# Reading the moving columns of every product as two halves in turn

## The chip, the cores and the metric

The kernel runs on one core of one Trainium2 chip. The metric is the device time of one execution, in microseconds (us). Engines are named as the profile names them: PE is TensorE (PEld its weight loads), DVE is VectorE, ACT is ScalarE, POOL is GpSimd, SP is SyncE, whose queue issues most DMAs.

## What is computed

One encoder layer on 512 tokens of width 1024, in float32. Two token mixers run side by side on the same input `h`, are merged by sigmoid gates, and a gated feed-forward net follows:

```python
proj = h @ w_in[l]
...
o_a = windowed_gqa_sink(qa, ka, va, a_sink[l]).astype(h.dtype)
o_b = dilated_mixture(qb, kb, vb).astype(h.dtype)
gates = jax.nn.sigmoid(h @ w_gate[l] + b_gate[l])
g_a, g_b = jnp.split(gates, N_BRANCH, axis=-1)
mixed = g_a * (o_a @ w_br_a[l]) + g_b * (o_b @ w_br_b[l])
y = mixed @ w_out[l]
h = layer_norm(DN_ALPHA * h + y, ln1_g[l], ln1_b[l])
f = (jax.nn.silu(h @ w_ff_gate[l]) * (h @ w_ff_up[l])) @ w_ff_down[l]
h = layer_norm(DN_ALPHA * h + f, ln2_g[l], ln2_b[l])
```

Mixer A has 16 query heads over 4 key heads and a window of 128 tokens to both sides. Mixer B has three groups of 4 heads with the window and dilation (128,1), (512,4) and (2048,16). The feed-forward width is 2816.

## The kernel before

**Split products.** Each float32 operand is cut into a high part `h` and a low part `l`, both of type float32r, by a copy (`copy`, L320 to L324, usually on ACT) and a subtraction (L348 and L371 on weights, L427 on `x`, L1213 later, all on DVE). A product is then three matmuls that add up in one PSUM bank: high by high, high by low, low by high. The stationary side has 128 columns (one weight load per matmul), the moving side 512 or 256. The places are these:

- `feat_k` (L442) multiplies weights by the moving tokens for projections, gates and the branch outputs: L452 to L454, 512 columns.
- `token_values` (L655) does it the other way round, tokens stationary and weights moving: L672 to L674.
- `scores` (L594, matmuls L601 and L602) and L828 make attention scores; L767, L768, L895 and L932 multiply probabilities with values.
- `tok_major` (L1098) does the output projection and the end of the down projection: L1110 to L1112.
- `Quad.product` (L1315) does gate and up projection, four 128-row steps at a time with 256 moving columns: L1323 to L1325. A block of 2 by 2 matrices takes seven products there, with sums of operands formed ahead and sums of results behind.
- `Chunk.step` (L1520) does most of the down projection in the same way: L1533 to L1535, 512 columns.

**Readers of PSUM.** `rotate` (L470: L472 and L474) applies the rotary turn; L750, L812, L835 and L838 add masks and take the row minimum; L779, L907 and L938 add two halves of an attention output; the gates are read at L958, the branch outputs at L1065 and L1077, layer norm sums at L1134; the quads copy (L322 on ACT, through `keep`), add (L1213, through `tt` and `plus`) and multiply (L1347, `minus_product`). Transposes on PE (L634, L701, L716, L1180) write banks that others read in plain order.

**Order.** The order on the engines is made when the program is built: `Program.run` (L167) is a list scheduler. Each `op` has a price (`act`, `dve` and `pe`, L268 to L277), a priority and the buffers that it holds; an operation starts on its engine when its inputs are priced as ready and its buffers fit, smallest priority first. Copies may go to ACT or DVE (`cp_alts`). The price of a matmul before is

```python
def pe(n):
    return max(0.109, 0.0133 + n / 2400)
```

in us for n moving columns. These prices decide the order, not the time on the chip. `copy`'s price for PSUM and `dve`'s price for 512 columns (0.60 us) are untouched by the change.

The work runs in this sequence: input, projections and both mixers, with gates in between (to 345 us), branch outputs (to about 400 us), output projection and layer norm (to about 460 us), the feed-forward quads and chunks (to about 745 us), the last of the down projection and the second layer norm.

Of the kernel before, what the change touches and what calls it, by code (L numbers as in the profile page):

```python
# [15 lines left out]
P = 128  # L16
# [259 lines left out]
def pe(n):  # L276
    return max(0.109, 0.0133 + n / 2400)  # L277
# [3 lines left out]
def hybrid_layer(ctx: ExitStack, tc: tile.TileContext, wpack, xT, xtok, sink, bgate,  # L281
# [134 lines left out]
    for j in range(KD):  # L416
        st, ap = slot(F32, "xs"), FIRST["x"][j]

        for c0, c1 in ((0, S // 2), (S // 2, S)) if j == 0 else ((0, S),):
            w, sk = c1 - c0, (st, c0)  # L420
            th, tl = [(b, j, c0) if j == 0 else (b, j) for b in (xh4[j // 4], xl4[j // 4])]
            eng, dma = (ACT, nc.scalar) if j == 0 and c0 == 0 else (SP, nc.sync)
            op([(eng, 0.4 if eng == ACT else 0.73 * w / S)], lambda e, j=j, st=st, dma=dma, c0=c0, c1=c1: dma.dma_start(
                st.t[:, c0:c1], xT[j, :, c0:c1]), writes=[sk], abs_prio=ap, moves=0.73 * w / S if eng == ACT else 0.0)
            op(cp_alts(w), lambda e, j=j, st=st, c0=c0, c1=c1: copy(e, xh[j]()[:, c0:c1], st.t[:, c0:c1]),
               reads=[sk], writes=[th], abs_prio=ap)
            op([(DVE, dve(w))], lambda e, j=j, st=st, c0=c0, c1=c1: nc.vector.tensor_tensor(  # L427
                xl[j]()[:, c0:c1], st.t[:, c0:c1], f32(xh[j]()[:, c0:c1]), op=ALU.subtract), reads=[sk, th],
               writes=[tl], abs_prio=ap)
# [12 lines left out]
    def feat_k(ps, wu, k, mov, toks, nk=KD, col=None, n0=0, n1=S, begins=True, split=False):  # L442
# [27 lines left out]
    def rotate(ps):  # L470
        R, Sh = slot(), slot()
        op([(DVE, dve(S))], lambda e: nc.vector.tensor_tensor(R.t, ps.t, cosT.t, op=ALU.mult),  # L472
           reads=[ps, cosT], writes=[R], prio=EV)
        op([(DVE, dve(S, extra=0.1))], lambda e: nc.vector.stream_shuffle(Sh.t, ps.t, SHUF), reads=[ps], writes=[Sh],  # L474
# [119 lines left out]
    def scores(o_of, q, qc, k, kc, n):  # L594
# [4 lines left out]
        def go():  # L599
            o = o_of()  # L600
            mm(o, qt.t[:, qc:qc + P], kt.t[:, kc:kc + n], start=True, stop=False, skip_group_check=True)  # L601
            mm(o, qt.t[:, qc:qc + P], kl.t[:, kc:kc + n], start=False, stop=True, skip_group_check=True)  # L602
# [4 lines left out]
    def turned_values(u, nt, turn_by=0, done=None):  # L607
# [3 lines left out]
        for i in range(2):  # L611
# [28 lines left out]
    def value_split(pb, c0=0):  # L640
# [3 lines left out]
        s = lambda: pb.t[:, c0:c0 + 256].rearrange("p (h c) -> p h c", h=4)  # L644
# [10 lines left out]
    def token_values(u):  # L655
# [11 lines left out]
        for k in range(KD):  # L667
            wh, wl = k_tile(k)
            for r, ps in enumerate(acc):
                def go(e, ps=ps, k=k, wh=wh, wl=wl, r=r):  # L670
                    a, b = xh[k]()[:, r * P:(r + 1) * P], xl[k]()[:, r * P:(r + 1) * P]
                    mm(ps.t, a, wh.t, start=(k == 0), stop=False)  # L672
                    mm(ps.t, a, wl.t, start=False, stop=False)
                    mm(ps.t, b, wh.t, start=False, stop=(k == KD - 1))  # L674
# [3 lines left out]
        for ps in acc:  # L678
            for g in range(2):
                res[g].append(value_split(ps, 256 * g))  # L680
# [53 lines left out]
    def unit_a(g, b, qs, kk, vs):  # L734
# [6 lines left out]
        for h in range(4):  # L741
# [9 lines left out]
                out=p.t[:, :n], in0=sb.t[:, :n], in1=mA.t[:, m0:m0 + n], scale=-0.125,  # L751
# [10 lines left out]
        for j, kb in enumerate(kbs):  # L762
            hh, ll = turned_probs([lambda h=h, j=j: ps_[h].t[:, j * P:(j + 1) * P] for h in range(4)], ps_)

            def pv(e, j=j, kb=kb, hh=hh, ll=ll):
                v = vs[kb].t.rearrange("p (h c) -> p h c", h=4)[:, g, :]
                mm(o.t, v, hh.t, start=(j == 0), stop=False)  # L767
                mm(o.t, v, ll.t, start=False, stop=(j == len(kbs) - 1))  # L768
# [3 lines left out]
        op(cp_alts(S, True), lambda e: copy(e, t.t[0:64], o.t[64:128]), reads=[o], writes=[t])  # L772

        def add(e):
            for h in range(4):
# [3 lines left out]
                nc.vector.tensor_tensor(dst, o.t[0:64, c].rearrange("p (r i) -> p r i", r=4),  # L779
# [4 lines left out]
    def unit_b(hs, q, k, v0, v1, v2):  # L784
# [12 lines left out]
        for half in range(2):  # L797
# [10 lines left out]
            for b in (2 * half, 2 * half + 1):  # L808
# [4 lines left out]
                       out=pn[half].t[:, c + w0:c + w1], in0=sb.t[:, c + w0:c + w1], in1=mB.t[:, w0:w1],  # L813
# [8 lines left out]
        for half in range(2):  # L822
            for r in (2 * half, 2 * half + 1):
                sb, c = bank("s"), (r % 2) * 256

                def go(e, sb=sb, r=r, c=c):
                    for g in (1, 2):
                        mm(sb.t[:, (g - 1) * 256:g * 256], q[g][0].t[:, r * P:(r + 1) * P],  # L828
                           k[g][r // 2].t[:, c:c + 256], start=True, stop=True, skip_group_check=True)
# [3 lines left out]
                two = lambda sb=sb: sb.t.rearrange("p (g a i) -> p g a i", g=2, a=2)  # L833
# [51 lines left out]
        for half in range(2):  # L885
# [5 lines left out]
            def pv(e, half=half, xs=xs, od=od):  # L891
                for n, x in enumerate(xs):
                    for g, vs in ((1, v1), (2, v2)):
                        v = vs[2 * half + n].t.rearrange("p (h c) -> p h c", h=4)[:, hs, :]
                        mm(od.t[:, n * 256:(n + 1) * 256], v, x.t[:, (g - 1) * 256:g * 256],  # L895
# [6 lines left out]
            part = lambda od=od: od.t.rearrange("p (r a i) -> p r a i", r=2, a=2)  # L902
# [50 lines left out]
    def gate(f, put=False):  # L953
# [4 lines left out]
        op([(ACT, act(S, True, 1))], lambda e: nc.scalar.activation(t.t, ps.t, AF.Identity, bias=bg.t[:, f:f + 1]),  # L958
# [101 lines left out]
    for f in range(8):  # L1060
# [4 lines left out]
        mark = op([(DVE, dve(S))], lambda e, f=f, ps=ps: nc.vector.tensor_tensor(gz[f].t, gz[f].t, ps.t, op=ALU.mult),  # L1065
# [5 lines left out]
    for f in range(8):  # L1071
# [5 lines left out]
        op([(DVE, dve(S))], lambda e, f=f, ps=ps: nc.vector.tensor_tensor(gz[8 + f].t, gz[8 + f].t, ps.t, op=ALU.mult),  # L1077
# [20 lines left out]
    def tok_major(nk, last, us_of, u0, g, b, finish, fine, alpha=ALPHA, between=None):  # L1098
# [4 lines left out]
        def kmm(k, t, j, c0, c1, us, wu):  # L1103
# [3 lines left out]
            def go(e):  # L1107
                a0, a1 = us[0].t[:, t * P:(t + 1) * P], us[1].t[:, t * P:(t + 1) * P]
                o = ps.t[:, c0:c1]
                mm(o, a0, wh.t[:, c0:c1], start=(k == 0), stop=False, skip_group_check=True)  # L1110
                mm(o, a0, wl.t[:, c0:c1], start=False, stop=False, skip_group_check=True)  # L1111
                mm(o, a1, wh.t[:, c0:c1], start=False, stop=(k == nk - 1), skip_group_check=True)  # L1112
# [11 lines left out]
        for t in range(NR):  # L1124
# [3 lines left out]
            for n, (j, c0, c1) in enumerate(pieces):  # L1128
                ps, z = acc[t, j], xt[t, j]
                for k, us, wu in res:  # L1130
# [4 lines left out]
                    z.t[:, c0:c1], z.t[:, c0:c1], alpha, ps.t[:, c0:c1], op0=ALU.mult, op1=ALU.add),  # L1135
# [541 lines left out]
```

## Time and profile before

| | |
|---|---|
| time, median of 3 runs (lowest, highest) | 787.1 us (786.98, 789.37) |
| the profiled execution, first to last instruction | 783.3 us; its time as the runs are timed is not listed apart |
| PE busy, matmul records | 770.7 us (98%), 4477 |
| DVE busy | 669.8 us (86%) |
| ACT busy | 448.8 us (57%) |
| granted clock of TensorE over the span | 0.997 |
| DMA | 124.89 MB, 159 GB/s in the mean |

A matmul's duration in the profile is longer than the distance to the next one, since matmuls are pipelined and their ends are modelled. What a matmul costs in a stream is read from the starts of its neighbours in the timeline. In the chain of waits, which follows the end of the program back to its start, a piece is charged only the time until the next piece begins.

### The profile page before, as it was taken

How to read it: one execution, taken by the hardware profiler on the slowest of the kernel's cores; microseconds unless marked ns; L12 is line 12 of the kernel's file. 1: busy time of each engine (PE TensorE's matmuls, PEld its weight loads, DVE VectorE, ACT ScalarE, POOL GpSimd, SP SyncE). 2: the span in 40 equal slices, each digit the busy share in tenths (PEclk: the TensorE clock that was granted, in tenths of full speed). 3: DMA queues.
4: the chain of work that ended last, by engine and by line, in shares of the span. 5: the costliest groups of instructions: out<-in, count | busy, mean ns of one | idle time of the engine just before them, and what ended most of it. 6: DMA issues, size and time to landing. Idle time of an engine off the chain costs nothing.

```text
span 783.3 us, 13444 instructions
## 1 busy us (share of the span) xinstructions
PE 770.7 (98%) x4477; PEld 677.5 (86%) x4477; DVE 669.8 (86%) x1445; ACT 448.8 (57%) x1009; POOL 103.5 (13%) x272
## 2 busy tenths in 40 slices
PE   9999999999999999999999999999999999999995
PEld 6888888888888888878878899999999999999984
DVE  5888998989697799578698898798998989898977
ACT  5656576765664663569433565656566555565710
POOL 0010000100002500340020011111112201212100
PEclk9999999999999999999999999999999999999998
DMA  8644543425527057649755368665977967967402
GB/s 273 222 124 136 133 123 95 121 87 157 158 64 210 27 137 194 182 162 311 230 116 137 81 212 193 162 162 149 230 226 184 223 160 201 239 168 177 106 28 80
DMA packets 71652, 124.89 MB, mean 159 GB/s; under 512 B 8864, under 2 KB 12832, under 8 KB 71584
## 3 DMA queue, kind: packets, MB, share of 16 engines
q1 hardware_dynamic: 61648, 106.08, 43.4%
q0 software_dynamic: 9792, 17.83, 14.1%
q8 instruction: 35, 0.57, 0.3%
q14 instruction: 33, 0.27, 0.1%
q10 hardware_dynamic: 144, 0.13, 0.0%
HBM read 105.40 MB, written 4.46 MB: 140 GB/s over the span
## 4 chain that ended last, share of the span: by engine, by line
PE 87%; DVE 7%; DMA 3%; ACT 2%; issue 1%; SPq 1%; DVEq 0%; ACTq 0%
PE ps L452 10%; PE ps L453 10%; PE ps L454 10%; PE ps L1323 9%; PE ps L1325 9%; PE ps L1324 9%; PE ps L1534 4%; PE ps L1533 4%; PE ps L1535 4%; PE ps L701 3%; PE ps L1110 2%; PE ps L1112 2%; PE ps L1111 2%; PE ps L602 1%; PE ps L601 1%
## 5 line engine op out<-in xcount | busy, mean ns | idle before, releaser
L322 ACT ACTIVATE sl<-sl 128x512 fp32r<-128x512 f32 (+3 forms) x397 | 218.5, 585 | 87.8 <-DVE sl L478 32.8
L1213 DVE TENSOR_TENSOR sl<-sl,sl 128x512 fp32r<-128x512 f32 (+3 forms) x294 | 166.4, 608 | 7.2 <-ACT sl L322 6.3
L322 ACT ACTIVATE sl<-ps 128x256 f32<-128x256 f32 (+4 forms) x195 | 83.9, 444 | 115.1 <-PE ps L1325 71.9
L452 PE MATMUL ps<-x,sl 128*128 128x512 f32 (+1 forms) x337 | 134.7, 400 | 0.0
L453 PE MATMUL ps<-x,sl 128*128 128x512 f32 (+1 forms) x337 | 132.2, 392 | 0.2 <-DVE x L427 0.2
L454 PE MATMUL ps<-x,sl 128*128 128x512 f32 (+1 forms) x337 | 131.6, 391 | 0.0
L1323 PE MATMUL ps<-sl,sl 128*128 128x256 f32 x352 | 99.8, 283 | 0.2 <-ACT sl L322 0.2
L348 DVE TENSOR_TENSOR sl<-sl,sl 128x512 fp32r<-128x512 f32 x130 | 87.3, 684 | 14.8 <-ACT sl L322 10.0
L1325 PE MATMUL ps<-sl,sl 128*128 128x256 f32 x352 | 99.6, 283 | 0.0
L1324 PE MATMUL ps<-sl,sl 128*128 128x256 f32 x352 | 99.6, 283 | 0.0
L454 PEld LDWEIGHTS ps<-x,sl 128*128 128x128 f32 x337 | 63.7, 189 | 13.7
L1323 PE MATMUL ps<-x,sl 128*128 128x256 f32 x264 | 74.7, 283 | 0.0
L1325 PE MATMUL ps<-x,sl 128*128 128x256 f32 x264 | 74.7, 283 | 0.0
L1324 PE MATMUL ps<-x,sl 128*128 128x256 f32 x264 | 74.7, 283 | 0.0
L453 PEld LDWEIGHTS ps<-x,sl 128*128 128x128 f32 x337 | 63.8, 189 | 11.1 <-DVE x L427 0.9
L452 PEld LDWEIGHTS ps<-x,sl 128*128 128x128 f32 x337 | 63.8, 189 | 10.8 <-ACT x L322 0.5
L336 POOL DMA_DIRECT2D sl<-wpack x44 | 39.3, 904 | 248.5 <-DMA sl<-wpack 107.7
L1323 PEld LDWEIGHTS ps<-sl,sl 128*128 128x128 f32 x352 | 67.5, 192 | 1.1 <-ACT sl L322 0.6
L1324 PEld LDWEIGHTS ps<-sl,sl 128*128 128x128 f32 x352 | 67.5, 192 | 0.4
L1325 PEld LDWEIGHTS ps<-sl,sl 128*128 128x128 f32 x352 | 67.5, 192 | 0.0
L1324 PEld LDWEIGHTS ps<-x,sl 128*128 128x128 f32 x264 | 50.6, 192 | 0.6
L1323 PEld LDWEIGHTS ps<-x,sl 128*128 128x128 f32 x264 | 50.6, 192 | 0.6
(143 smaller groups left out, 1598.3 us busy)
## 6 DMA issues: line engine op xcount, KB each, us to landing
sl<-wpack SPq DMA_DIRECT2D x243, 256.0 KB, 3.8
sl<-sl SPq DMA_DIRECT2D x108, 128.0 KB, 2.3
wf<-wpack SPq DMA_DIRECT2D x51, 256.0 KB, 4.8
sl<-wpack POOLq DMA_DIRECT2D x44, 256.0 KB, 5.6
wf<-wpack POOLq DMA_DIRECT2D x24, 256.0 KB, 5.2
gz<-sl SPq DMA_DIRECT2D x9, 256.0 KB, 2.2
sl<-gz SPq DMA_DIRECT2D x9, 256.0 KB, 5.1
sl<-xtok SPq DMA_DIRECT2D x8, 256.0 KB, 5.6
```

The lines of the kernel that those rows point to most:

```text
L322: nc.scalar.activation(dst, src, AF.Copy)
L336: op([(POOL, 1.0)], lambda e: nc.gpsimd.dma_start(b.t, src2, accum_op=ALU.add), reads=[b], writes=[b], prio=prio, moves=1.65)
L348: op([(DVE, dve(S))], lambda e: nc.vector.tensor_tensor(l.t, src.t, f32(h.t), op=ALU.subtract), reads=[src, h], writes=[l], prio=prio, abs ...
L452: mm(o, a, x0, start=(k == 0 and begins), stop=False, skip_group_check=split)
L453: mm(o, a, x1, start=False, stop=False, skip_group_check=split)
L454: mm(o, b, x0, start=False, stop=(k == nk - 1), skip_group_check=split)
L1213: op([(DVE, dve(w))], lambda e: nc.vector.tensor_tensor(dst(), x(), y(), op=o), reads=reads, writes=writes, prio=prio)
L1323: mm(o, wh, bh[k](), start=(first and k == 0), stop=False, skip_group_check=True)
L1324: mm(o, wh, bl[k](), start=False, stop=False, skip_group_check=True)
L1325: mm(o, wl, bh[k](), start=False, stop=(k == 3), skip_group_check=True)
L1533: mm(ps.t, x0, w[0].t, start=(first and m == 0), stop=False, skip_group_check=True)
L1534: mm(ps.t, x0, w[1].t, start=False, stop=False, skip_group_check=True)
```

## The change

Every matmul of a product, except the windowed value product L932, reads its moving columns in another order: instead of columns 0, 1, 2, ... it reads column 0, column n/2, column 1, column n/2 + 1, and so on. Three helpers make the access patterns: `pairs` for the matmul's moving operand, `back` for a PSUM result (its columns now stand with a step of two), `halves` for a tile in SBUF that is read or written along with such a result as two runs. The matmul writes its PSUM columns one after the other as before, so a bank now holds the result shuffled; whoever reads the bank puts it right by reading with a step of two elements. Stationary operands, weight loads, the number of matmuls, and every transpose are as before. `pe`, the scheduler's price, is changed with it.

```diff
 def pe(n):
-    return max(0.109, 0.0133 + n / 2400)
+    return max(0.109, 0.0026 + n / 2390)
+def pairs(ap):
+    return ap.rearrange("p (a b) -> p b a", a=2)
+def back(ap):
+    return ap.rearrange("p (b a) -> p a b", a=2)
+def halves(ap):
+    return ap.rearrange("p (a b) -> p a b", a=2)
...
+            cut = lambda ap, c0=c0, c1=c1: halves(ap)[:, :, c0 // 2:c1 // 2]
...
-                st.t[:, c0:c1], xT[j, :, c0:c1]), writes=[sk], abs_prio=ap, moves=0.73 * w / S if eng == ACT else 0.0)
+                cut(st.t), cut(xT[j])), writes=[sk], abs_prio=ap, moves=0.73 * w / S if eng == ACT else 0.0)
...
-            x0, x1 = mh()[:, n0:n1], ml()[:, n0:n1]
+            x0, x1 = [pairs(m())[:, n0 // 2:n1 // 2] for m in (mh, ml)]
...
-        op([(DVE, dve(S))], lambda e: nc.vector.tensor_tensor(R.t, ps.t, cosT.t, op=ALU.mult),
+        op([(DVE, dve(S))], lambda e: nc.vector.tensor_tensor(halves(R.t), back(ps.t), halves(cosT.t), op=ALU.mult),
...
             def evac(e, t=t, ps=ps):
-                s = view(ps.t, nt, True)
-                if turn_by:
-                    copy(e, view(t.t[:, turn_by * w:], nt - turn_by, False), s[:, :nt - turn_by])
-                    copy(e, view(t.t[:, :turn_by * w], turn_by, False), s[:, nt - turn_by:])
-                else:
-                    copy(e, view(t.t, nt, False), s)
-            op(cp_alts(S, True), evac, reads=[ps], writes=[t], prio=EV)
+                for a in range(2):
+                    s = ps.t.rearrange("p (r t i a) -> p a t r i", a=2, r=2, t=nt)[:, a]
+                    d = t.t.rearrange("p (t a r i) -> p a t r i", a=2, r=2, t=nt)[:, a]
+                    if turn_by:
+                        copy(e, d[:, turn_by:], s[:, :nt - turn_by])
+                        copy(e, d[:, :turn_by], s[:, nt - turn_by:])
+                    else:
+                        copy(e, d, s)
+            op(cp_alts(S, True, 0.3 if turn_by else 0.1), evac, reads=[ps], writes=[t], prio=EV)
...
-                out=p.t[:, :n], in0=sb.t[:, :n], in1=mA.t[:, m0:m0 + n], scale=-0.125,
+                out=halves(p.t[:, :n]), in0=back(sb.t[:, :n]), in1=halves(mA.t[:, m0:m0 + n]), scale=-0.125,
...
-                    mm(o, wh, bh[k](), start=(first and k == 0), stop=False, skip_group_check=True)
+                    mm(o, wh, pairs(bh[k]()), start=(first and k == 0), stop=False, skip_group_check=True)
...
-            copy_by_act(lambda: dst.t[:, c], lambda: ps.t[:, pc], HP, True, [(ps, tok)], [(dst, n)],
+            copy_by_act(lambda: halves(dst.t[:, c]), lambda: back(ps.t[:, pc]), HP, True, [(ps, tok)], [(dst, n)],
...
-                        mm(ps.t, x0, w[0].t, start=(first and m == 0), stop=False, skip_group_check=True)
+                        mm(ps.t, x0, pairs(w[0].t), start=(first and m == 0), stop=False, skip_group_check=True)
...
-                        tt(lambda z=z: z.t, lambda z=z: z.t, lambda ps=ps: ps.t, o, [z, ps], [z], S)
+                        tt(lambda z=z: halves(z.t), lambda z=z: halves(z.t), lambda ps=ps: back(ps.t), o, [z, ps], [z], S)
```

All other matmuls and PSUM readers listed above change in the same manner. For the first tile of `x`, which comes in two DMAs of 256 columns, each DMA now brings columns 0 to 127 and 256 to 383, or the other half of each. In the program of the change all lines stand 14 to 20 further down (L322 is L336, L1077 is L1096, L1347 is L1366).

Since the prices changed, the list scheduler orders the same operations a little differently. Three places show how. On ACT, soon after the start, between weight copies (`sl` from `sl`) stands the evacuation of the first value projection from its bank; before:

```order
L322 ACTIVATE sl_279<-sl_194 128x512
L322 ACTIVATE sl_289<-sl_217 128x512
L322 ACTIVATE sl_298<-sl_231 128x512
L322 ACTIVATE sl_302<-ps_163 128x512
L322 ACTIVATE sl_307<-sl_238 128x512
```

and now:

```order
L336 ACTIVATE sl_282<-sl_197 128x512
L336 ACTIVATE sl_292<-sl_217 128x512
L336 ACTIVATE sl_298<-ps_162 128x4x64 x2
L336 ACTIVATE sl_302<-sl_231 128x512
L336 ACTIVATE sl_313<-sl_238 128x512
```

The evacuation has become two copies of half the width and stands one weight copy earlier. On DVE, in the branch outputs, each gated sum takes a product from PSUM (L1077, now L1096), a sum (L1079, L1098) and the low part for the output projection (L1035, L1054); before:

```order
L1077 TENSOR_TENSOR sl_3903<-sl_3903,ps_4767 128x512
L1035 TENSOR_TENSOR sl_4805<-sl_4236,sl_4804 128x512
L1079 TENSOR_TENSOR sl_4244<-sl_4244,sl_3903 128x512
L1035 TENSOR_TENSOR sl_4820<-sl_4238,sl_4819 128x512
L1077 TENSOR_TENSOR sl_3909<-sl_3909,ps_4780 128x512
L1035 TENSOR_TENSOR sl_4839<-sl_4244,sl_4838 128x512
L1079 TENSOR_TENSOR sl_4246<-sl_4246,sl_3909 128x512
L1077 TENSOR_TENSOR sl_4004<-sl_4004,ps_4799 128x512
```

and now:

```order
L1096 TENSOR_TENSOR sl_3863<-sl_3863,ps_4771 128x512
L1054 TENSOR_TENSOR sl_4815<-sl_4236,sl_4814 128x512
L1054 TENSOR_TENSOR sl_4822<-sl_4238,sl_4821 128x512
L1098 TENSOR_TENSOR sl_4240<-sl_4240,sl_3863 128x512
L1096 TENSOR_TENSOR sl_3914<-sl_3914,ps_4785 128x512
L1096 TENSOR_TENSOR sl_4021<-sl_4021,ps_4810 128x512
L1054 TENSOR_TENSOR sl_4850<-sl_4240,sl_4849 128x512
L1098 TENSOR_TENSOR sl_4242<-sl_4242,sl_3914 128x512
```

The last two products from PSUM follow each other, and one low part stands ahead of a sum instead of behind it. On DVE in the feed-forward stage, where a quad ends (the two products L1347, now L1366, one of an SBUF tile and one of a bank) and a chunk's result is added to the tokens (L1213 from `ps`, now L1232); before:

```order
L1213 TENSOR_TENSOR sl_6573<-sl_6573,ps_6557 128x512
L1213 TENSOR_TENSOR sl_6663<-sl_6312,sl_6662 128x512
L1213 TENSOR_TENSOR sl_6628<-sl_6628 128x256
L1347 SCALAR_TENSOR_TENSOR sl_6573<-sl_6573,sl_6628 128x256
L1347 SCALAR_TENSOR_TENSOR sl_6573<-sl_6573,ps_6538 128x256
L1213 TENSOR_TENSOR sl_6691<-sl_6330,sl_6690 128x512
```

and now:

```order
L1232 TENSOR_TENSOR sl_6562<-sl_6562,ps_6536 128x512
L1232 TENSOR_TENSOR sl_6683<-sl_6312,sl_6682 128x512
L1232 TENSOR_TENSOR sl_6638<-sl_6638 128x256
L1366 SCALAR_TENSOR_TENSOR sl_6562<-sl_6562,ps_6451 128x256
L1366 SCALAR_TENSOR_TENSOR sl_6562<-sl_6562,sl_6638 128x256
L1232 TENSOR_TENSOR sl_6695<-sl_6330,sl_6694 128x512
```

The two products change places, so that the one that frees the bank comes first. Over the whole program PE has the same number of instructions. The four evacuations of value projections for turning have six copies more in all, on ACT or DVE; nothing else is added.

More of the change, by code (lines that the diff above doesn't have):

```diff
@@ L420, in hybrid_layer @@
             w, sk = c1 - c0, (st, c0)
+            cut = lambda ap, c0=c0, c1=c1: halves(ap)[:, :, c0 // 2:c1 // 2]
             th, tl = [(b, j, c0) if j == 0 else (b, j) for b in (xh4[j // 4], xl4[j // 4])]
             eng, dma = (ACT, nc.scalar) if j == 0 and c0 == 0 else (SP, nc.sync)
-            op([(eng, 0.4 if eng == ACT else 0.73 * w / S)], lambda e, j=j, st=st, dma=dma, c0=c0, c1=c1: dma.dma_start(
-                st.t[:, c0:c1], xT[j, :, c0:c1]), writes=[sk], abs_prio=ap, moves=0.73 * w / S if eng == ACT else 0.0)
-            op(cp_alts(w), lambda e, j=j, st=st, c0=c0, c1=c1: copy(e, xh[j]()[:, c0:c1], st.t[:, c0:c1]),
+            op([(eng, 0.4 if eng == ACT else 0.73 * w / S)], lambda e, j=j, st=st, dma=dma, cut=cut: dma.dma_start(
+                cut(st.t), cut(xT[j])), writes=[sk], abs_prio=ap, moves=0.73 * w / S if eng == ACT else 0.0)
+            op(cp_alts(w), lambda e, j=j, st=st, cut=cut: copy(e, cut(xh[j]()), cut(st.t)),
                reads=[sk], writes=[th], abs_prio=ap)
-            op([(DVE, dve(w))], lambda e, j=j, st=st, c0=c0, c1=c1: nc.vector.tensor_tensor(
-                xl[j]()[:, c0:c1], st.t[:, c0:c1], f32(xh[j]()[:, c0:c1]), op=ALU.subtract), reads=[sk, th],
+            op([(DVE, dve(w))], lambda e, j=j, st=st, cut=cut: nc.vector.tensor_tensor(
+                cut(xl[j]()), cut(st.t), cut(f32(xh[j]())), op=ALU.subtract), reads=[sk, th],
                writes=[tl], abs_prio=ap)
@@ L471, in rotate @@
         R, Sh = slot(), slot()
-        op([(DVE, dve(S))], lambda e: nc.vector.tensor_tensor(R.t, ps.t, cosT.t, op=ALU.mult),
+        op([(DVE, dve(S))], lambda e: nc.vector.tensor_tensor(halves(R.t), back(ps.t), halves(cosT.t), op=ALU.mult),
            reads=[ps, cosT], writes=[R], prio=EV)
-        op([(DVE, dve(S, extra=0.1))], lambda e: nc.vector.stream_shuffle(Sh.t, ps.t, SHUF), reads=[ps], writes=[Sh],
+        op([(DVE, dve(S, extra=0.1))], lambda e: nc.vector.stream_shuffle(halves(Sh.t), back(ps.t), SHUF), reads=[ps], writes=[Sh],
            prio=EV)
@@ L766, in pv @@
                 v = vs[kb].t.rearrange("p (h c) -> p h c", h=4)[:, g, :]
-                mm(o.t, v, hh.t, start=(j == 0), stop=False)
-                mm(o.t, v, ll.t, start=False, stop=(j == len(kbs) - 1))
+                mm(o.t, v, pairs(hh.t), start=(j == 0), stop=False)
+                mm(o.t, v, pairs(ll.t), start=False, stop=(j == len(kbs) - 1))
             op([(PE, 2 * pe(S))], pv, reads=[hh, ll, *vtok(vs[kb])], writes=[o])
         t = slot(F32, "att")
-        op(cp_alts(S, True), lambda e: copy(e, t.t[0:64], o.t[64:128]), reads=[o], writes=[t])
+        op(cp_alts(S, True), lambda e: copy(e, halves(t.t[0:64]), back(o.t[64:128])), reads=[o], writes=[t])
         def add(e):
```

79 lines of the change are left out of this document (41 added, 38 removed).

## Prediction

> **What bounds the kernel now.** I read the page's busy shares first, then its chain of waits, then stretches of the span, and last the starts of neighbouring matmuls in the timeline. The first two, from the page:
>
> ```profile
> PE 770.7 (98%) x4477; PEld 677.5 (86%) x4477; DVE 669.8 (86%) x1445; ACT 448.8 (57%) x1009; POOL 103.5 (13%) x272
> ...
> PE 87%; DVE 7%; DMA 3%; ACT 2%; issue 1%; SPq 1%; DVEq 0%; ACTq 0%
> ```
>
> PE is busy nearly always, and 87% of the chain that ended last is matmuls. Busy PE alone would not prove a bound, since matmul records overlap; so the next view, busy time by stretches, with the columns PE, PEld, DVE, ACT, POOL, then granted clock, DMA share and GB/s:
>
> ```profile
> 25.00:345.00 320.00, 319.65 (x1608) 269.83 (x1607) 269.21 (x694) 191.56 (x465) 42.91 (x192) 1.00 0.47 135
> ...
> 464.00:480.00 16.00, 15.79 (x131) 15.59 (x131) 15.61 (x35) 11.85 (x25) 5.30 (x6) 1.00 1.05 287
> 480.00:745.00 265.00, 265.00 (x1901) 250.97 (x1900) 236.04 (x446) 158.98 (x346) 45.15 (x52) 1.00 0.72 181
> ...
> 764.00:783.30 19.30, 11.02 (x49) 8.81 (x47) 15.60 (x29) 0.88 (x3) 0.00 (x0) 0.87 0.22 82
> ```
>
> Projections and mixers (25 to 345 us) and the feed-forward net (480 to 745) hold three quarters of the span, and PE has hardly a gap in them. DVE is at 84% and 89%: the second engine, and close.
>
> **What one matmul costs.** In the timeline of PE, first and last of a run of 512-column matmuls (23 rows, 22 steps), then of a run of 256-column ones (52 rows, 51 steps); the columns are start, duration, what:
>
> ```profile
> 29.77 0.39 PE L453 MATMUL ps<-x,sl 128*128 128x512 f32 x1
> ...
> 34.76 0.39 PE L454 MATMUL ps<-x,sl 128*128 128x512 f32 x1
> ```
>
> ```profile
> 499.78 0.28 PE L1325 MATMUL ps<-sl,sl 128*128 128x256 f32 x1
> ...
> 505.90 0.28 PE L1325 MATMUL ps<-x,sl 128*128 128x256 f32 x1
> ```
>
> The starts are (34.76 − 29.77)/22 = 0.2268 us apart at 512 columns and (505.90 − 499.78)/51 = 0.1200 us at 256. The difference, 106.8 ns for 256 columns, is 0.417 ns a column; 512 × 0.417 = 213.5, so **13.3 ns of each matmul do not depend on its columns**. The scheduler's old price, 0.0133 + n/2400, is the same line (226.6 and 120.0 ns): it was drawn through this behaviour. The new price, 0.0026 + n/2390, gives 216.8 and 109.7 ns. That says what the new reading would have to do, take away 10.7 of the 13.3 ns; it shows nothing.
>
> **The sum.** The matmuls that change, from the groups by line and shape (each L452, L1323, L1533 and L1110 row stands for three lines of equal count, the L672 row for three, the L767 row for two):
>
> ```profile
> L452 PE MATMUL ps<-x,sl 128*128 128x512 f32 x335 | 133.5, 398 | 0.0
> ...
> L1323 PE MATMUL ps<-sl,sl 128*128 128x256 f32 x352 | 99.8, 283 | 0.2 <-ACT sl L322 0.2
> ...
> L1323 PE MATMUL ps<-x,sl 128*128 128x256 f32 x264 | 74.7, 283 | 0.0
> ...
> L1533 PE MATMUL ps<-sl,sl 128*128 128x512 f32 x126 | 49.3, 391 | 0.0
> ...
> L1110 PE MATMUL ps<-sl,sl 128*128 128x512 f32 x96 | 38.1, 396 | 1.4 <-DVE sl L1077 1.2
> ...
> L452 PE MATMUL ps<-sl,sl 128*128 128x512 f32 x80 | 31.5, 393 | 0.0
> ...
> L672 PE MATMUL ps<-sl,x 128*128 128x512 f32 x32 | 12.9, 402 | 0.0
> ...
> L767 PE MATMUL ps<-sl,sl 128*128 128x512 f32 x40 | 15.6, 390 | 0.0
> ```
>
> That is 3 × (335 + 126 + 96 + 80 + 32) + 80 = 2087 of 512 columns and 3 × 616 = 1848 of 256; in the code stand some 150 more of 256 and 64 of 384 (scores, dilated values). At the claimed prices: 2087 × 9.9 = 20.7 us, 2000 × 10.3 = 20.6, 64 × 10 = 0.6, together **41.9 us off PE**.
>
> Whether a matmul can get that cheap: the transposes, with a weight load each and 128 columns, set one floor in the trace, eight in 0.87 us of the chain, 109 ns each:
>
> ```profile
> 57.31 0.87 PE ps L701 x8
> ```
>
> So 109.7 ns for a matmul and its weight load has a neighbour at 109; less than that at 256 columns I do not expect. **The unknown price has these ends**: below, the whole fixed term goes at 512 columns (213.5) and 109 remains at 256, 2087 × 13.3 + 2000 × 11 = 49.8 us off; above, the same transposes read 128 columns at 109/128 = 0.85 ns a column, the dearest reading in the trace, and at that rate 512 columns take 435 ns and 256 take 218, which adds 2087 × 208 + 2000 × 98 = 630 us. No row shows columns read with a jump each. I take 216.8 and 109.7, close to the lower end: the transposes are bounded by 128-column weight loads as much as by their moving side, so their price per column is a poor neighbour, while the 512-column rows show the streaming itself at 0.417 ns and 13.3 ns of something else beside it.
>
> [...]
>
> **What of it reaches the end.** The chain is 87% PE; in the other 13% (the loads at the start, some stretches of DVE, the tail) a faster PE only waits longer. I count 41.9 × 0.87 = **36.5 us**; all 41.9 is the bound above.
>
> The second stretch gets tightest: there PE has about 1557 matmuls of 256 columns (three lines of 519) and 342 of 512; they save 16.0 + 3.4 = 19.4 us, so 265 becomes 245.6 against 236 us of DVE, 96%. The first has 1608 − 272 unchanged (transposes, L932) = 1336, saves 13.3, and 306.7 faces 269, 88%. I cost this at nothing: in 464 to 480 us DVE is at 15.61 of 16 us and PE still runs 15.79. DMA goes from 0.72 to 0.78 in the second stretch, and 1.05 stands in that same short one. If DVE's cover fails there, the 9.6 us between 236 and 245.6 are what is left before DVE sets the pace.
>
> **The readers of PSUM.** The operations stay what they are, with a step of two on one operand. Neighbours are reads cut into short runs: L502 reads and writes runs of 32 columns, L579 runs of 128; the first row is the same operation on whole rows:
>
> ```profile
> L1213 DVE TENSOR_TENSOR sl<-sl,sl 128x512 f32<-128x512 f32 x48 | 32.4, 685 | 0.5
> ...
> L502 DVE TENSOR_TENSOR sl<-sl,sl 64x512 fp32r<-64x512 f32 x2 | 1.4, 685 | 0.0
> ...
> L579 DVE TENSOR_TENSOR sl<-sl,sl 128x256 fp32r<-128x256 f32 x8 | 3.0, 420 | 0.0
> ...
> L1213 DVE TENSOR_TENSOR sl<-sl,ps 128x512 f32<-128x512 f32 x53 | 36.2, 685 | 12.8 <-PE ps L1535 9.0 <-PE ps L1325 2.9
> ```
>
> Runs cost nothing (685 against 685), nor does PSUM as a source. A gain is excluded, because DVE already takes one column at a time: (685 − 420)/256 = 1.04 ns each. A loss is not: 0 to one more such step, 1.04 ns per column read. I take 0, by the rows of runs. ACT, 57% busy, has room for either. From the code, DVE reads about 69,000 columns so in the first stretch (44 × 512 in the rotations, 32 × 384 + 32 × 256 in masks, the rest in unit sums) and 36,000 in the second (42 × 512 chunk sums, 19 × 768 in quads).
>
> The rest is small. Four evacuations of values become two or four copies each, six extra starts of some 0.1 us on ACT or DVE beside a streaming PE; if uncovered, under 1 us. The first tile of `x` arrives in shorter runs while PE still warms up; the same bound. Reordered operations on DVE (the branch outputs) sit in the 13% that I do not count.
>
> **Forecast.** The profile's span is 783.3 us and its 3.8 us distance to the median of 787.1 is taken as what lies around it. 783.3 − 36.5 + 3.8 = 750.6, that is 751.
>
> **Rivals.**
> - *The step of two costs DVE time.* With p ns per column, the second stretch needs 236 + 36p against PE's 245.6, the first 269 + 69p against 306.7: DVE takes over from p = 0.27 and 0.55. At p = 0.55 the second is 255.8, 10 us later than forecast: 761. At p = 1.04 they are 273.4 and 340.8, 8 and 21 us over before, and with the 9.2 us gained elsewhere at most (41.9 less these two stretches' 32.7): 807, **slower**. It turns to slower at about p = 0.88, where both overruns and that gain cancel. For it: DVE is close; against it: the rows of runs. [...]
> - *The 13.3 ns stay*, since they belong to the matmul and not to the order of columns. Then only order and copies change: 787.
> - *Each jump costs PE.* From a price above 226.8 and 120.0 ns it is a loss, since PE has no gap to hide it; at 0.85 ns a column 787 + 630 = 1417 us, and any smaller price in between.
>
> **Chances.** Forecast 0.68 (own range 743 to 758: the whole 41.9 or a little more reaches the end, or some 7 us go to DVE); DVE costs part of it, 757 to 780, 0.14; DVE costs more than all, 0.03; no change 0.04; PE dearer 0.11. The range 743 to 778 takes in the first two, 0.8 of it. Within 0.3% (2.4 us, about what a measurement of this kernel can tell from no change) lies the fourth alone: faster 0.82, same 0.04, slower 0.14.
>
> **What would show it.** In the timeline after, starts 0.217 us apart at 512 columns and 0.110 at 256 make the sum right; 0.227 and 0.120 make the second rival right; more, the third. The group L1213 of `sl` and `ps` at 685 ns and L472 at the same say that the step is free; 950 or more say that it is not. In 480 to 745 us, the chain says whether DVE has come in between matmuls. The forecast is wrong above all if the fixed term is not what the reading order touches.

## The result and the profile after

The changed kernel takes **748.55 us** (median of 4 runs, 746.57 to 751.01), the kernel before beside it 787.04 us (4 runs, 786.37 to 789.37). The ratio is 0.951, 95% interval 0.949 to 0.954: 38.5 us less. The profiled execution took 751.01 us, the longest of the four; its span is 749.2 us.

The page of the changed kernel, busy time and the chain of waits:

```profile
PE 730.4 (97%) x4477; PEld 664.5 (89%) x4477; DVE 662.9 (88%) x1445; ACT 447.7 (60%) x1015; POOL 104.2 (14%) x272
...
PE 87%; DVE 6%; DMA 3%; ACT 1%; issue 1%; SPq 1%; DVEq 0%; ACTq 0%
```

PE still sets the end with the same 87%, and DVE's work has not grown (669.8 us before, 662.9 now). So the time went out of the matmuls. The timeline of PE, first and last row of 26 with 512 columns (25 steps), then of 24 with 256 columns (23 steps):

```profile
29.26 0.38 PE L468 MATMUL ps<-x,sl 128*128 128x512 f32 x1
...
34.66 0.38 PE L469 MATMUL ps<-x,sl 128*128 128x512 f32 x1
...
446.48 0.28 PE L1342 MATMUL ps<-sl,sl 128*128 128x256 f32 x1
...
449.05 0.28 PE L1344 MATMUL ps<-sl,sl 128*128 128x256 f32 x1
```

The starts are 5.40/25 = 0.2160 us and 2.57/23 = 0.1117 us apart; before it was 0.2268 and 0.1200, and 0.2168 and 0.1097 were forecast. Taken over all neighbours between 25 and 725 us (waits, and single steps more than a tenth above the usual, left out), the mean went from 228.4 to 216.0 ns at 512 columns, from 119.8 to 111.7 ns at 256, and from 175.9 to 162.5 ns at 384. At 512 columns the mean before is above the 226.8 ns of the run that the prediction read, because some starts stood 231 to 236 ns apart, most of them among the first four of a run of such matmuls; those are gone too.

The groups of DVE that now read PSUM with a step of two (mean ns of one is the number behind the busy time):

```profile
L1232 DVE TENSOR_TENSOR sl<-sl,ps 128x512 f32<-128x512 f32 x53 | 36.0, 684 | 12.3 <-PE ps L1555 8.3 <-PE ps L1344 3.4
...
L768 DVE CUSTOM_DVE_ANT_0 sl<-ps,sl,nsink 128x384 f32<-128x384 f32 x32 | 19.1, 612 | 2.5 <-PE ps L617 2.5
...
L489 DVE STREAM_SHUFFLE sl<-ps 128x512 f32<-128x512 f32 x22 | 16.1, 734 | 0.0
L487 DVE TENSOR_TENSOR sl<-ps,sl 128x512 f32<-128x512 f32 x22 | 15.0, 684 | 2.8 <-PE ps L469 2.6
```

Before, two of these groups (L768 was L750, L489 was L474; L1213 stands in the prediction):

```profile
L750 DVE CUSTOM_DVE_ANT_0 sl<-ps,sl,nsink 128x384 f32<-128x384 f32 x32 | 19.3, 611 | 1.9 <-PE ps L602 1.8
L474 DVE STREAM_SHUFFLE sl<-ps 128x512 f32<-128x512 f32 x22 | 16.2, 736 | 0.0
```

684 ns where the same group L1213 took 685 before: the step costs nothing. DVE is now very full in the feed-forward net, and PE has no gap all the same (busy time by stretches, columns as in the prediction):

```profile
500.00:600.00 100.00, 100.00 (x755) 95.90 (x754) 97.38 (x190) 60.27 (x132) 20.79 (x24) 1.00 0.82 211
```

What was lost again stands in two views: the waits of PE from 25 us on (us in total, times, longest), and the timeline at 35 us with the stretches around it and around the gates:

```profile
PE ps L651 <- ACT sl L336: 2.2, 1, 2.2
PE ps L467 <- ACT sl L336: 1.8, 1, 1.8
PE ps L1342 <- ACT sl L336: 1.8, 1, 1.8
PE ps L1129 <- DVE sl L1096: 1.6, 1, 1.6
```

```profile
34.87 0.27 PE L651 MATMUL ps<-ident,sl 128*128 128x128 f32 x1
37.32 0.55 PE L651 MATMUL ps<-ident,sl 128*128 128x128 f32 x3 [2.18 <-ACT sl L336]
...
41.00 0.63 PE L469 MATMUL ps<-x,sl 128*128 128x512 f32 x1
41.43 0.63 PE L467 MATMUL ps<-x,sl 128*128 128x512 f32 x1
```

```profile
36.00:48.00 12.00, 10.68 (x48) 9.31 (x49) 9.00 (x21) 5.92 (x16) 0.96 (x3) 0.86 0.22 80
330.00:345.00 15.00, 12.89 (x69) 10.84 (x68) 11.78 (x33) 13.06 (x28) 0.00 (x0) 0.89 0.26 86
```

PE waits at 35 us for the evacuated values that the transposes at L651 turn, and a little later its matmuls stand 0.43 us apart, twice the usual: the granted clock is 0.86 in that stretch and 0.89 in the second. Closer windows show it halved for 3.4 us in each, so each such piece costs 1.7 us:

```profile
38.70:42.10 3.40, 3.40 (x12) 2.75 (x11) 1.74 (x4) 1.97 (x5) 0.00 (x0) 0.50 0.07 28
335.70:339.00 3.30, 3.17 (x10) 2.61 (x11) 1.86 (x6) 3.16 (x8) 0.00 (x0) 0.50 0.17 54
```

The kernel before had 1.00 in both stretches, and of its waits of PE after 25 us only one was above 0.5 us:

```profile
PE ps L1110 <- DVE sl L1077: 1.2, 1, 1.2
```

What the transposes at L651 wait for stands in ACT's timeline:

```profile
35.58 1.15 ACT L336 ACTIVATE sl<-sl 64x512 fp32r<-64x512 f32 x2 [1.42 <-DVE sl L493]
36.64 0.63 ACT L336 ACTIVATE sl<-ps 128x256 f32<-128x256 f32 x2
```

The second row is the evacuation, and the transposes start as it ends, at 37.3 us. It stands on ACT behind two copies that wait 1.42 us for DVE's rotary sum (L493). So the lateness comes from the place in ACT's order, not from the cut into two copies: as one copy it takes 0.58 us (with the same order in the first experiment, and at 23.18 us in the kernel before) instead of 0.63.

### The profile page after: what moved, and what is told of

Same layout as the page of the kernel before. It is cut to its first block, busy times and chain, and to the rows that moved or that the text cites. A ratio compares the mean times of both kernels' runs of the same rounds, so it can differ in the third digit from the quotient of the medians.

```text
span 749.2 us, 13499 instructions
## 1 busy us (share of the span) xinstructions
PE 730.4 (97%) x4477; PEld 664.5 (89%) x4477; DVE 662.9 (88%) x1445; ACT 447.7 (60%) x1015; POOL 104.2 (14%) x272
## 4 chain that ended last, share of the span: by engine, by line
PE 87%; DVE 6%; DMA 3%; ACT 1%; issue 1%; SPq 1%; DVEq 0%; ACTq 0%
PE ps L468 10%; PE ps L469 10%; PE ps L467 10%; PE ps L1343 9%; PE ps L1342 9%; PE ps L1344 9%; PE ps L1555 4%; PE ps L1553 4%; PE ps L1554 4%; PE ps L719 3%; PE ps L1129 2%; PE ps L1131 2%; PE ps L1130 2%; DMA sl<-wpack 1%; PE ps L617 1%; PE ps L616 1%
## 5 line engine op out<-in xcount | busy, mean ns | idle before, releaser
L336 ACT ACTIVATE sl<-sl 128x512 fp32r<-128x512 f32 (+3 forms) x395 | 216.5, 584 | 84.7 <-DVE sl L493 31.3
L1232 DVE TENSOR_TENSOR sl<-sl,sl 128x512 fp32r<-128x512 f32 (+3 forms) x294 | 165.5, 607 | 3.5 <-ACT sl L336 3.0
L336 ACT ACTIVATE sl<-ps 128x256 f32<-128x256 f32 (+5 forms) x205 | 86.0, 437 | 104.0 <-PE ps L1344 60.4
L467 PE MATMUL ps<-x,sl 128*128 128x512 f32 (+1 forms) x337 | 130.4, 387 | 0.3 <-ACT x L336 0.3
L468 PE MATMUL ps<-x,sl 128*128 128x512 f32 (+1 forms) x337 | 128.4, 381 | 0.5 <-DVE x L442 0.4
L469 PE MATMUL ps<-x,sl 128*128 128x512 f32 (+1 forms) x337 | 128.1, 380 | 0.0
L1342 PE MATMUL ps<-sl,sl 128*128 128x256 f32 x352 | 96.9, 275 | 1.8 <-ACT sl L336 1.8
L1343 PE MATMUL ps<-sl,sl 128*128 128x256 f32 x352 | 96.8, 275 | 0.0
L1344 PE MATMUL ps<-sl,sl 128*128 128x256 f32 x352 | 96.8, 275 | 0.0
L1342 PE MATMUL ps<-x,sl 128*128 128x256 f32 x264 | 72.6, 275 | 0.0
L1343 PE MATMUL ps<-x,sl 128*128 128x256 f32 x264 | 72.6, 275 | 0.0
L1344 PE MATMUL ps<-x,sl 128*128 128x256 f32 x264 | 72.6, 275 | 0.0
L467 PEld LDWEIGHTS ps<-x,sl 128*128 128x128 f32 x337 | 64.3, 191 | 8.4 <-ACT x L336 0.7
L1342 PEld LDWEIGHTS ps<-sl,sl 128*128 128x128 f32 x352 | 67.6, 192 | 2.1 <-ACT sl L336 2.0
L1342 PEld LDWEIGHTS ps<-x,sl 128*128 128x128 f32 x264 | 50.6, 192 | 0.4
```

The costliest lines, as they stand in the source:

```text
L336: nc.scalar.activation(dst, src, AF.Copy)
L467: mm(o, a, x0, start=(k == 0 and begins), stop=False, skip_group_check=split)
L468: mm(o, a, x1, start=False, stop=False, skip_group_check=split)
L469: mm(o, b, x0, start=False, stop=(k == nk - 1), skip_group_check=split)
L1232: op([(DVE, dve(w))], lambda e: nc.vector.tensor_tensor(dst(), x(), y(), op=o), reads=reads, writes=writes, prio=prio)
L1342: mm(o, wh, pairs(bh[k]()), start=(first and k == 0), stop=False, skip_group_check=True)
```

## Experiments

In the experiments on reading orders the lines stand four further down (L467 is L471), and six matmuls at the start, those of the first tile of `x` with 256 columns, keep the halves in turn. Where one time is given without a range, it is that of a single execution. Two theories said why the order of columns matters. **A**: the 13.3 ns belong to two neighbouring columns following each other, so any order that avoids this saves them. **B**: they belong to where the columns come from, and two places taken in turn, far apart, are what helps (B1); or to the form of the access pattern as such (B2).

### The new order of instructions alone

```diff
 def pe(n):
-    return max(0.109, 0.0133 + n / 2400)
+    return max(0.109, 0.0026 + n / 2390)
```

This is the kernel before with only the price changed.

> The kernel before with the new price of a matmul alone (0.0026 + n/2390), so the scheduler's order of the change and nothing else of it. If the gain is in the matmul (my theory), starts stay 226.8 and 120 ns apart and the time stays within 3 us of 787. If the new order brings the gain (rival), it is near 749.

Measured: 787.17 us (786.34 to 788.05), ratio 1.0011, interval 1.0001 to 1.0020. Rows of its timeline (21 steps), and its waits of PE:

```profile
29.13 0.39 PE L454 MATMUL ps<-x,sl 128*128 128x512 f32 x1
...
33.89 0.39 PE L454 MATMUL ps<-x,sl 128*128 128x512 f32 x1
```

```profile
PE ps L452 <- ACT sl L322: 1.7, 1, 1.7
PE ps L1323 <- ACT sl L322: 1.5, 1, 1.5
PE ps L1110 <- DVE sl L1077: 1.2, 1, 1.2
```

Starts are 4.76/21 = 0.2267 us apart, as before. The order gains nothing by itself. It loses 0.2% at most, and it brings two of the waits of after along: those of L452 and L1323 are 1.7 and 1.5 us here, where the kernel before has none of L452 and 0.2 us of L1323.

### The readers alone

```diff
 def pairs(ap):
-    return ap.rearrange("p (a b) -> p b a", a=2)
+    return ap
```

The changed kernel with moving columns read one after the other; order, copies and steps of two in the readers stay.

> The changed kernel, but the matmuls read columns one after the other, while the readers of PSUM keep their step of two and the order of instructions stays that of the change; its results stand in the wrong columns. If the reading order of the moving columns is the cause, starts go back to 226.8 and 120 ns and the time to 785 to 790 (order and stepped readers cost nothing), and to over 792 if the stepped readers cost something that the faster PE hid. If the step at the readers or the order is the cause, it stays near 749.

Measured: 787.34 us (785.76 to 788.32), ratio 1.0009, interval 1.0000 to 1.0019; starts 4.53/20 = 0.2265 us apart:

```profile
29.29 0.39 PE L472 MATMUL ps<-x,sl 128*128 128x512 f32 x1
...
33.82 0.39 PE L471 MATMUL ps<-x,sl 128*128 128x512 f32 x1
```

So the whole gain, 787.3 to 748.6 us, is the matmul's reading order.

### A step of two

```diff
 def pairs(ap):
-    return ap.rearrange("p (a b) -> p b a", a=2)
+    return ap.rearrange("p (b a) -> p a b", a=2)
```

> The changed kernel, but the moving columns are read even ones first, then odd ones (a step of 8 bytes, one stream); results in the wrong columns. Theory A (the fixed term is there whenever the next column read is the neighbour of the last): 216 and 112 ns as in the change, about 749. Theory B (two distant places have to be read in turn): 226.8 and 120, about 787. A penalty for a jump at every column: over 800.

Measured: 1470.92 us (before: 786.7); 15 steps:

```profile
28.89 0.63 PE L473 MATMUL ps<-x,sl 128*128 128x512 f32 x1
...
35.69 0.63 PE L473 MATMUL ps<-x,sl 128*128 128x512 f32 x1
```

0.4533 us from start to start, twice the plain read, although no two neighbours follow each other: avoiding neighbours is not enough, and A falls.

### Runs of two, runs of four, quarters

Three more orders: halves in turn two columns at a time (0, 1, 256, 257, ...), four columns at a time, and four quarters in turn (0, 128, 256, 384, 1, ...).

```diff
-    return ap.rearrange("p (a b) -> p b a", a=2)
+    return ap.rearrange("p (a b c) -> p b a c", a=2, c=2)   # runs of two
+    return ap.rearrange("p (a b c) -> p b a c", a=2, c=4)   # runs of four
+    return ap.rearrange("p (a b) -> p b a", a=4)            # quarters
```

Runs of two:

> The changed kernel, but the halves are read in turn two columns at a time; results in the wrong columns. Theory A (every neighbour read costs): half of the reads are neighbours, so something between, 220 and 116 ns, about 768, or 787 if any neighbour is enough. Theory B (two distant places in turn): 216 and 112, about 749.

Runs of four:

> The changed kernel, but the halves are read in turn four columns (16 bytes) at a time; results in the wrong columns. Step of two gave 451 ns at 512 columns and runs of two 330, halves column by column 216. Theory B1 (only a change of place on every column is quick, and each run of neighbours in a broken stream costs by the number of breaks): half the breaks of runs of two, so between 226 and 330 ns, about 275, and 900 to 960 us. Theory B2 (a short inner dimension of the access pattern decides, not the places): 330 or more.

Quarters:

> The changed kernel, but four quarters of the columns are read in turn, column by column (0, n/4, n/2, 3n/4, 1, ...); results in the wrong columns. Theory B1 (a far change of place on every column): 216 and 112 ns, about 749. If exactly two streams are needed (a place for each of two, not four): 400 ns or more at 512 columns, over 1300.

Measured: 1095.81 us (before 786.7), 845.41 and 941.47 us (before 785.96). Timelines in this order, 20, 27 and 24 steps:

```profile
29.28 0.50 PE L473 MATMUL ps<-x,sl 128*128 128x512 f32 x1
...
35.94 0.50 PE L472 MATMUL ps<-x,sl 128*128 128x512 f32 x1
```

```profile
29.24 0.41 PE L472 MATMUL ps<-x,sl 128*128 128x512 f32 x1
...
35.99 0.42 PE L472 MATMUL ps<-x,sl 128*128 128x512 f32 x1
```

```profile
29.18 0.45 PE L473 MATMUL ps<-x,sl 128*128 128x512 f32 x1
...
35.98 0.45 PE L473 MATMUL ps<-x,sl 128*128 128x512 f32 x1
```

0.333, 0.250 and 0.283 us. All are dearer than the plain read, though each changes place often and far. No expectation had runs of two above 787 us, quarters fit neither of their two, and runs of four stayed below the 900 us that B1 gave. It is not jumping as such that helps, so B1 is too wide: two places, and one column from each.

### Two places, near and far

```diff
-    return ap.rearrange("p (a b) -> p b a", a=2)
+    return ap.rearrange("p (k a b) -> p k b a", a=2, b=16)  # 64 bytes apart
+    return ap.rearrange("p (k a b) -> p k b a", a=2, b=4)   # 16 bytes apart
+    return ap.rearrange("p (k a b) -> p k b a", a=2, b=2)   # 0, 2, 1, 3: 8 bytes apart
```

64 bytes:

> The changed kernel, but the two places read in turn are 16 columns (64 bytes) apart, in groups of 32; results in the wrong columns. [...] If the distance has to be that of another memory block (512 bytes or more): 330 to 450 ns and over 1100.

16 bytes:

> The changed kernel with the two places that a moving read takes in turn only four columns (16 bytes) apart: columns 0, 4, 1, 5, 2, 6, 3, 7, then the next eight. Its columns come out in another order than the readers expect, so the output stands in the wrong columns; the work is the same. If what counts is that two neighbours in the order come from two different pieces of 16 bytes (the reading that fits e8_in_one_line, where 0, 2, 1, 3 within 16 bytes ran like the contiguous read), starts of 512 columns stand 216 ns apart and of 256 columns 112, and the run takes about 750 us. If the piece is 32 bytes or more, both places lie in one piece, starts stand 227 and 120 ns apart, and the run takes 787 to 789 us. If the read must stay in each of its two places for a long run, the jump every eight columns costs, and the time lies above 789 us, towards the 845 us of runs of four.

8 bytes, within 16:

> The changed kernel, but columns are exchanged within groups of four only (0, 2, 1, 3, 4, 6, 5, 7, ...: 16 bytes); results in the wrong columns. Theory B1 (the two places have to be far apart): slow, 330 to 450 ns at 512 columns, 1100 to 1470 us. Theory B2 (the form of the access pattern, inner dimension of two, decides): 216, about 749. [...]

Measured: 750.0 us (before 785.96), 748.11 us (before 786.05) and 789.12 us (before 785.96). Timelines in this order, 28, 26 and 29 steps:

```profile
29.16 0.38 PE L472 MATMUL ps<-x,sl 128*128 128x512 f32 x1
...
35.20 0.38 PE L473 MATMUL ps<-x,sl 128*128 128x512 f32 x1
```

```profile
29.25 0.38 PE L471 MATMUL ps<-x,sl 128*128 128x512 f32 x1
...
34.87 0.38 PE L473 MATMUL ps<-x,sl 128*128 128x512 f32 x1
```

```profile
29.24 0.39 PE L471 MATMUL ps<-x,sl 128*128 128x512 f32 x1
...
35.81 0.39 PE L473 MATMUL ps<-x,sl 128*128 128x512 f32 x1
```

0.2157, 0.2162 and 0.2266 us. B2 falls with the last one: the form of the pattern is that of the other two, and it runs like the plain read. Nor need the places be far apart: 16 bytes do. Among the orders that take one column from each of two places, the fixed term is there at 8 bytes (0.2266 us) and gone at 16, 64 and 1024 (0.2162, 0.2157, 0.2160). Two neighbours out of two different pieces of 16 bytes, as the expectation for 16 bytes has it, would fit these four, and so would a mere distance of 16 bytes or more; no run tells the two apart, and none shows why.

### What holds the 256-column matmuls at 111.7 ns

```diff
-                    mm(o, wh, pairs(bh[k]()), start=(first and k == 0), stop=False, skip_group_check=True)
-                    mm(o, wh, pairs(bl[k]()), start=False, stop=False, skip_group_check=True)
-                    mm(o, wl, pairs(bh[k]()), start=False, stop=(k == 3), skip_group_check=True)
+                    m = HP if first and k == 0 else 192
+                    mm(o[:, :m], wh, pairs(bh[k]()[:, :m]), start=(first and k == 0), stop=False, skip_group_check=True)
+                    mm(o[:, :192], wh, pairs(bl[k]()[:, :192]), start=False, stop=False, skip_group_check=True)
+                    mm(o[:, :192], wl, pairs(bh[k]()[:, :192]), start=False, stop=(k == 3), skip_group_check=True)
```

> The changed kernel, but the gate and up product reads only 192 of its 256 moving columns, except in the first matmul of each bank; a quarter of that product's columns is left out (its output is only partly summed). About 1770 of the 1848 matmuls of that product become 64 columns narrower. If the 111.65 ns from start to start of 256 columns are a floor that the weight load or the issue sets, the narrower ones keep 111 to 112 ns and the run takes 745 to 751 us. If the 111.65 ns are streaming time plus a fixed 5 ns (256 times 0.417 is 106.7), 192 columns take 80 + 5 = 85 ns, PE sheds 1770 times 26.7 = 47 us, and with the vector engine at 99% in that stretch the run ends somewhere from 705 to 740 us.

Measured: 750.27 us (before 786.05), although a quarter of the columns of most of these matmuls is gone. Its timeline, from a bank's first matmul on:

```profile
441.04 0.30 PE L1343 MATMUL ps<-sl,sl 128*128 128x256 f32 x1
441.18 0.25 PE L1344 MATMUL ps<-sl,sl 128*128 128x192 f32 x1
441.27 0.28 PE L1345 MATMUL ps<-sl,sl 128*128 128x192 f32 x1
...
445.96 0.28 PE L1345 MATMUL ps<-sl,sl 128*128 128x192 f32 x1
```

From 441.27 to 445.96 us there are 42 steps of 0.1117 us: 192 columns cost what 256 cost. Just behind a wider matmul one step is only 0.09 us (441.18 to 441.27), but the wider one before it took 0.14, and together they come to two steps of the stream, so this step alone prices nothing. In the stream something other than the columns sets 111.7 ns for each matmul. Every one has a weight load of 128 columns, and in such a stream of the changed kernel (428 to 445 us, 152 loads) PEld is busy 16.97 of 17.00 us; that the loads are the floor is an estimate from this, since no run took them away.

### Repeated, and with a later place for the transposes

The changed kernel once more:

> The changed kernel unaltered, beside the two others of this chip: 747 to 751 us. The matmul engine's wait of 2.2 us at 35 us of the span, and the halved clock that follows it, appear again if they belong to the kernel and not to one execution.

And a version with the price as measured and a later place for the transposes that waited:

```diff
 def pe(n):
-    return max(0.109, 0.0026 + n / 2390)
+    return max(0.1117, 0.0026 + n / 2400)
...
-            op([(PE, 0.18)], turn, reads=[*src, ident], writes=[pb])
+            op([(PE, 0.18)], turn, reads=[*src, ident], writes=[pb], prio=4.0)
```

> The changed kernel with the two numbers that its planner goes by corrected to what was measured (the floor of a matmul 111.7 ns in place of 109, the slope 1/2400 in place of 1/2390), and the first transposes at L651, which waited 2.2 us for the scalar engine's copy, given a later place in the order (9 matmuls later on the matmul engine). If the wait at 35 us and the half clock after it (3.4 us of records at half clock, so about 1.7 us lost) are a cost of this order, both go and the run takes 744 to 747 us. If the half clock comes at some point whatever the order, or if the wait shows up at another place, it takes 747 to 751 us like the changed kernel.

Measured on one chip: the changed kernel 747.67 us (747.39 to 748.89), ratio 0.9513 (0.9500 to 0.9526); the other version 746.87 us (746.38 to 748.05), ratio 0.9503 (0.9490 to 0.9516). The intervals overlap, so that version is not shown to be faster; and it changes the price and the place together, so their shares are not told apart. The stretches of the repeated kernel, then of the other version with its timeline at the gates:

```profile
36.00:48.00 12.00, 11.06 (x58) 9.89 (x59) 10.56 (x25) 7.06 (x19) 1.15 (x4) 1.00 0.28 92
330.00:345.00 15.00, 12.89 (x72) 10.96 (x71) 13.33 (x32) 14.87 (x32) 0.00 (x0) 1.00 0.46 141
```

```profile
33.00:48.00 15.00, 15.00 (x78) 13.30 (x77) 14.76 (x33) 9.13 (x22) 0.77 (x4) 1.00 0.46 140
325.00:345.00 20.00, 16.37 (x95) 14.37 (x94) 15.92 (x40) 17.69 (x40) 0.00 (x0) 0.91 0.41 132
```

```profile
333.01 0.65 PE L467 MATMUL ps<-sl,sl 128*128 128x512 f32 x1 [3.56 <-ACT sl L336]
```

Two things follow. The repeated kernel pauses at the same two places, 1.3 us at 35 us (2.2 in the first profile) and 1.8 at the gates (1.8), and has no halved clock behind either (1.00 and 1.00, where the first profile had 0.86 and 0.89); its span is 745.8 us against 749.2, a difference as large as two pieces of 1.7. So the halved clock follows a pause in some executions and not in others. In the first profile two of its four pauses of 1.6 to 2.2 us are followed by such a piece, those at 35 us and at the gates; behind the 1.6 us at L1129 (388 to 400 us) and the 1.8 us at L1342 (698.6 to 710 us) the clock is 1.00. What decides it no run shows.

And the later transposes take the wait at 35 us away (PE busy 15.00 of 15.00), but the wait at the gates grew from 1.8 to 3.6 us, and the granted clock over that stretch is 0.91. It ends at the same moment, 333.01 us, where it ends at 333.05 in the repeated kernel: PE waits there for the high part of a weight, whose copy on ACT stands behind a table load and two sigmoids of the gates (L1066; 1.28 and 1.15 us in the first profile after), at the same time in both. What PE gained at 35 us it waited away at the gates.

## Why the prediction was right, point by point

**The bound.** Right: PE set the end, and the time that its matmuls lost left the span. The size came out well, 750.6 us against 748.55, with some luck: several terms were off in ways that cancel.

**The sum was right as a whole, with two terms off to opposite sides.** At the measured means, 2087 × (228.4 − 216.0) = 25.9 us came from 512 columns where 20.7 were forecast: the claimed price 216.8 was nearly met (216.0), but the run that was read for the price of before, 226.8, left out the starts at 231 to 236 ns. From 256 columns came 2000 × (119.8 − 111.7) = 16.2 us where 20.6 were forecast. Here the step "109.7 ns has a neighbour at 109" failed: the transposes' 109 ns is not the floor of these matmuls, 111.7 is, and the narrower product showed that 192 columns do not go below it. That the transposes are bounded by their weight loads as much as by their moving side was the author's estimate; no run shows it. With 64 × 13.4 = 0.9 us at 384 columns the sum is 43.0 us, where 41.9 were forecast.

**The share that reaches the end.** 43.0 × 0.87 = 37.4 us; the spans are 34.0 us (with both halved pieces) and 37.5 us shorter, the medians 38.5 and 38.4 us. The factor held as a number, but not as the even share that it was taken for. In the quads (first matmul to last, 443.56 to 742.04 us before, 424.76 to 704.37 in the repeated kernel) 18.9 us arrive of the 19 that the measured prices give there, so nearly all. Behind them nothing arrives of about 1.9: that tail takes 41.2 us before and 41.4 after. Ahead of them 18.8 us of about 22.4 arrive, and what is missing there is mostly new waits of PE, which the prediction counted at nothing.

Of these waits, the four of the first profile after add up to 7.4 us, where those of before with 0.5 us or more were 1.2 and 0.5 us. Two of the new ones come with the order alone. The one at L651 comes with the faster matmuls: it is at most 0.2 us in the runs whose 512 columns take 227 ns or more, and it is there in each of those where they take 216 (2.2, 1.3, 2.0 and 1.3 us; 1.4 with the narrow product), as long as the transposes keep their place. PE is there sooner, and the evacuation on ACT is not: it starts at 35.9 us with the order alone, at 36.6 and 36.3 us in the two profiles of the changed kernel. The prediction had named the evacuation's extra copies, at under 1 us; they cost 0.05 us here, and the wait has another source.

**What lies around the span.** The prediction took 3.8 us, the distance of a profile's span from a median of other executions. In each run whose span is listed the distance is 1.7 to 2.0 us, so this term was about 2 us too large; by them the profile before was of a quick execution, of some 785 us.

**DVE's cover held.** The forecast was 96% in the feed-forward stretch; over the quads, first matmul to last, DVE went from 90% to 94%, in the fullest 100 us after it is at 97.4 and PE at 100.0. The quads went from 298.5 to 279.6 us, 18.9 us less, where 19.4 were forecast for 265 us of them.

**The readers.** Right at 0 ns per column: 684 against 685 ns, 612 against 611, 734 against 736. The first rival, with 761 and 807 us, falls: none of these prices of a step is seen in PSUM. (One sum in it is off: by its own figures slower began where 105p − 80 = 9.2, at p = 0.85 and not 0.88. Nothing else rests on it.)

**The second rival, 787 us** (the 13.3 ns belong to the matmul), falls: its time is what plain reading gives, 787.3, with all else as in the change, so most of the fixed term goes with the reading order.

**The third rival.** For this order it is wrong, and for others right: with a step of two 1470.92 us, more than the bound of 1417. Nor does the number of jumps order these runs: halves in turn, quarters and a step of two all jump at every column, at 0.216, 0.283 and 0.453 us for 512 columns; runs of two jump at every second column and take 0.333, runs of four at every fourth and take 0.250; and 0, 2, 1, 3, which jumps in three steps of four, takes the 0.227 of the plain reading. The inner cause is not shown and stays open.

## What to carry to other kernels

Read the fixed part of a matmul's price from two widths in the timeline; where it is as large as the 13.3 ns here, try the order in which the moving columns are read before anything else, and put the result right in whoever reads PSUM, which cost nothing here (684 ns against 685). Of the orders tried, only two places 16, 64 or 1024 bytes apart, one column each, gave the gain (0.2157 to 0.2162 us); a step of two nearly doubled the kernel's time (1470.92 us), so measure the exact order. When the bounding engine gets faster, look for the producers whose slack was smaller than the gain: here an evacuation on ACT, behind copies that wait for DVE, became a wait of PE.

## What the hardware showed that was not expected

- Where moving columns of float32r come from sets the price of a column over a factor of two: 0.216 us for 512 columns in the best order, 0.227 plain, 0.453 with a step of two.
- 192 and 256 moving columns cost the same 111.7 ns in a stream of matmuls with a weight load each.
- A pause of PE of 1.8 us at the gates was followed by 3.4 us of half clock in one execution and not in another of the same kernel (granted clock 0.89 and 1.00 over 330 to 345 us); in the first of them two of four pauses of 1.6 to 2.2 us were.
